# Near-diagonal score levels of a gated linear recurrence computed in blocks of 32 tokens instead of 128

## The chip, the core and the metric

The kernel runs on one core of one Trainium2 chip. The core has a matrix engine (TensorE; PE in the profile, its weight loads PEld), a vector engine (VectorE, DVE), an activation engine (ScalarE, ACT), a general engine (GpSimd, POOL) and a queue that issues transfers (SyncE, SP). Matrix products are written to PSUM, which TensorE alone fills and which DVE and ACT read; everything else lives in SBUF, 128 partitions wide, or in HBM, reached by DMA. The metric is the device time in microseconds of one execution, the median of several.

## The reference, cut to what matters

The program is one layer of a decoder over 16 meta tokens and 1024 tokens (1040 in all), of width 1024: a mixer, and then a gated MLP with a short convolution. Half of the mixer is a gated linear recurrence with 4 heads, keys of 128 and values of 128. The change is in its scores:

```python
def _hgrn2_chunk_step(state, xs):
    q, k, v, lf = xs
    b = jnp.cumsum(lf, axis=2)
    o_inter = jnp.einsum('bhtk,bhkv->bhtv', q * jnp.exp(b), state)
    diff = b[:, :, :, None, :] - b[:, :, None, :, :]
    decay = jnp.where(causal, jnp.exp(jnp.where(causal, diff, 0.0)), 0.0)
    scores = jnp.einsum('bhtk,bhtsk,bhsk->bhts', q, decay, k)
    o_intra = jnp.einsum('bhts,bhsv->bhtv', scores, v)
    k_dec = k * jnp.exp(b_last[:, :, None, :] - b)
    new_state = jnp.exp(b_last)[..., None] * state + jnp.einsum('bhsk,bhsv->bhkv', k_dec, v)
    return new_state, o_inter + o_intra
```

The decay between a query t and an earlier key s is different in each of the 128 key channels, so the scores aren't one matrix product. Outside this function stand the projections that give q, the forget gate, the values and the gates; a causal pooling branch; two branch projections; an output projection; and the MLP.

## The kernel before, in words

**The scores by levels.** The kernel takes chunks of P = 128 tokens, NCH = 8 of them behind the meta tokens. Inside a chunk it splits the pairs (t, s) by levels 2, 4, 8, 16, 32 and 64. At level lv the tokens are cut into blocks of 2·lv; the second half of a block holds queries, the first half keys, and both are scaled by the decay from the block's middle. So one tile holds scaled keys and scaled queries interleaved, and a product of it with itself has the wanted scores in some places. What the levels leave (the diagonal and its direct neighbour) is the base, a product of keys and queries.

**Scores on TensorE (`head_steps`).** For levels 2 to 16 `level_mm` makes for each chunk one product of all 128 columns of the chunk (as weights) with its 64 query columns (L833), 8 of them into one bank of PSUM, 128x512. `level_out` picks the wanted places out of it with one predicated copy on DVE through a mask of bytes (L849, 128x512 elements), into the head's score array `sc`, 128x1024, that POOL has set to zero (L803). For levels 32 and 64 each product is made for the wanted block alone: weights 32 or 64 columns wide, written at partitions 0 and 64, or at 0 (L829); a plain copy on ACT or DVE sets them into `sc` (L843; the list `ON_ACT` says which are ACT's). The base is 8 products of 128 by 128 per head (L890), in two banks, with one predicated copy of 128x512 for each bank (L891). One product in float32 shows in the trace as two weight loads and two matmuls. Later steps of the head make the states (L899, L906), and the outputs from `sc` and the values, and from the states (L928, L929).

**What the levels get.** Cumulated logarithms `b` come from a scan on DVE: for heads 0 and 1 nine scans of a chunk each (L673), for heads 2 and 3 one scan over 1040 elements with an array `keep_on` that is zero where a chunk begins (L669). A level's tile then takes a subtraction (L750), two exponentials on ACT (L753, L754) and two products with q and k (L756, L757). Heads 0 and 1 have this done early, by `prepare`, during the gate projections, and stored to HBM (`hscr`); `head_steps` loads the tiles again (L691). Heads 2 and 3 do it in place. The list `POOLED` says which of these operations go to POOL; the others go to DVE.

**Order.** After the gate projections the work follows the list `ORDER`: `p1` is a step of `prepare`, `F2` the forget-gate projection of head 2 (`Fa2`, `Fb2` its two halves), `c2` its chain of logarithms, `Q..` the query projection, `h0` the next of the 12 or 13 steps of head 0, `l`, `w` loads and early weight splits of later stages, `BB0..7` and `BA0..7` the two branch projections, `sa` the split of a head's output. Inside this stage the program order is the list's, and a planner with its own costs places the instructions on the engines' queues; SP's queue issues in order. A `BB` result with more than SPILL_OVER = 4 `h` steps behind it in the list is stored to HBM (L1372) and loaded again for its `BA` (L1358). Large tiles come from a pool of 27 slots.

Of the kernel before, what the change touches and what calls it, by code (L numbers as in the profile page):

```python
# [41 lines left out]
LUP = 2.0 ** 60  # L42
KT = 6
HT = 514
HN = HT - HALO
# [16 lines left out]

ORDER = ("p1 p1 p1 p1 h0 F2 p1 h0 p1 h0 p1 Qa2 p1 p1 p1 p1 p1 h0 h0 c2 h1 w1 Qb2 h0 w0 Fa3 h1 h0 h2 h0 h0 h2 w4 h1 "
         "h0 h1 h1 h2 l0 Fb3 w4 c3 h1 h0 Q3 h0 h2 h2 h1 h3 h1 w4 l1 h2 h2 l2 l3 h1 h1 w2 h3 BB0 h2 h2 h3 h2 w5 BB1 "
         "h3 h1 BB2 h3 BB3 w5 h1 h3 BB4 h3 h2 BB5 w3 sa1 h3 h3 h3 sa0 h2 BB6 h3 h1 w5 h2 BB7 sa2 w5 h3 sa3 BA1 BA5 "
         "BA6 BA2 BA4 h3 BA0 BA3 BA7")
POOLED = ("e1k.0 e1k.3 kdsub.2 lk32.1 lk4.1 lq32.1 lq64.3 lq8.0 osg.2 wBA2 wBA6 wBA7 wBB2 wF0 wF3 wPP2 wPV0 wPV1 "
          "wQ0 qsmul.1 lq2.1 wQ2 sub2.3 lk32.3 lq4.2 sub8.0 lq32.0 lk64.1 sub8.3 lk2.1 qsmul.0 sub4.2 lq8.3 lq32.3 "
          "lk16.1 lq2.0 lk8.1 sub32.2 lf.1 lq4.3 sub4.1 e1q.2 sub2.0 qsmul.3 lq4.0 lk8.3 sub64.1 lq8.2 lq4.1 sub2.2 "
          "lk4.2 e1k.2 e1k.1 wQ3 kdsub.1").split()  # L70
ON_ACT = "lo32.0 lo32.1 lo64.0 lo64.1 lo32.2 lo64.2 lo64.3".split()
SPILL_OVER = 4
# [8 lines left out]
def trunk_kernel(ctx: ExitStack, tc: tile.TileContext, x, meta_tokens, mix_norm_pre,  # L81
# [523 lines left out]
    masks = {}  # L605
    mbase = const.tile([P, P], U8, name="mbase")
    mtmps = slot(P + len(LEVELS) * P // 2, name="mtmps")
# [5 lines left out]
                         pattern=[[2, P // 2], [1, 2]], channel_multiplier=-1)  # L613
    pool_e.tensor_copy(mbase, mtmp)
    for i, h in enumerate(LEVELS):
# [6 lines left out]
        masks[h] = const.tile([P, P // 2], U8, name=f"mask{h}")  # L622
        pool_e.tensor_copy(masks[h], mt)

# [32 lines left out]
    def chain_steps(h, kk, b, f, f2):  # L657
# [9 lines left out]
        eng(f"lf.{h}").tensor_tensor(f, f, f2, ALU.add)  # L667
        if ("F", h) not in FIRST_JOBS:
            dve.tensor_tensor_scan(b, keep_on[0], f, 0.0, ALU.mult, ALU.add)  # L669
        else:  # L670
            for lo in range(NM - P, L, P):
                t = slice(max(lo, 0), lo + P)
                dve.tensor_tensor_scan(b[:, t], ones[:, : t.stop - t.start], f[:, t], 0.0, ALU.mult, ALU.add)  # L673
        heads[h].update(kk=kk, b=b, f=f)
# [114 lines left out]
    def head_steps(h):  # L789
# [11 lines left out]
        if early:  # L801
            q = load_part("q", h)
        pool_e.memset(sc, 0.0)  # L803

        def meta_mm():
# [15 lines left out]
        def level_mm(lv, qk):  # L821
            ps = bank("sl")
            half = lv >= 32
            for c in range(NCH):
                t = NM + c * P
                if half:
                    for i in range(P // (2 * lv)):
                        s, n = t + 2 * lv * i, 2 * lv * i
                        pe.matmul(ps[n : n + lv, c * lv : (c + 1) * lv], qk[:, s : s + lv], qk[:, s + lv : s + 2 * lv],  # L829
                                  start=True, stop=True)  # L830
                    continue
                rhs = qk[:, t : t + P].rearrange("p (b two h) -> p b two h", two=2, h=lv)[:, :, 1, :]
                pe.matmul(ps[:, c * 64 : (c + 1) * 64], qk[:, t : t + P], rhs, start=True, stop=True)  # L833
            return ps

        def level_out(lv, ps):
# [8 lines left out]
            nb = P // (2 * lv)  # L845
            o4 = sc.rearrange("p (c b two h) -> p c b two h", c=NCH, two=2, h=lv)[:, :, :, 1, :]
            p4 = ps.rearrange("p (c b h) -> p c b h", c=NCH, h=lv)
            m4 = masks[lv].rearrange("p (o b h) -> p o b h", o=1, h=lv).to_broadcast([P, NCH, nb, lv])
# [36 lines left out]
        yield  # L885
        for j in range(2):
            ps = bank("sb")
            for i in range(4):
                t = NM + (4 * j + i) * P
                pe.matmul(ps[:, i * P : (i + 1) * P], kk[:, t : t + P], q[:, t : t + P], start=True, stop=True)  # L890
            dve.copy_predicated(sc[:, j * 512 : (j + 1) * 512].rearrange("p (c t) -> p c t", c=4),  # L891
                                mbase.rearrange("p (o t) -> p o t", o=1).to_broadcast([P, 4, P]),
                                ps.rearrange("p (c t) -> p c t", c=4))
        yield
# [1078 lines left out]
```

## Time and profile before

| | |
|---|---|
| median of 3 runs | 1338.39 us (1337.05 to 1339.64) |
| the profiled execution | 1341.08 us, its span 1339.2 us |
| mean granted TensorE clock | 0.993 |
| TensorE busy | 1319.1 us (98%), 7665 matmuls |
| DVE, ACT, POOL busy | 991.3, 610.5, 466.2 us |
| mean DMA traffic | 207 GB/s |
| stage of the heads | about 357 to 590 us of the span |

The row of a group has the line, the engine, the operation, the tile written and read, the shapes and the count; then busy time, mean duration of one, and the idle time before them with what ended it. In a row of the timeline or of the chain stand the start and the length of a run of like instructions; matmuls are pipelined, so a run's length is the spacing of the starts times their number, and a little more. The chain is followed back from the last instruction to what released it.

### The profile page before, as it was taken

How to read it: one execution, taken by the hardware profiler on the slowest of the kernel's cores; microseconds unless marked ns; L12 is line 12 of the kernel's file. 1: busy time of each engine (PE TensorE's matmuls, PEld its weight loads, DVE VectorE, ACT ScalarE, POOL GpSimd, SP SyncE). 2: the span in 40 equal slices, each digit the busy share in tenths (PEclk: the TensorE clock that was granted, in tenths of full speed). 3: DMA queues.
4: the chain of work that ended last, by engine and by line, in shares of the span. 5: the costliest groups of instructions: out<-in, count | busy, mean ns of one | idle time of the engine just before them, and what ended most of it. 6: DMA issues, size and time to landing. Idle time of an engine off the chain costs nothing.

```text
span 1339.2 us, 20195 instructions
## 1 busy us (share of the span) xinstructions
PE 1319.1 (98%) x7665; PEld 1166.1 (87%) x7665; DVE 991.3 (74%) x1260; ACT 610.5 (46%) x985; POOL 466.2 (35%) x348
## 2 busy tenths in 40 slices
PE   8999999999999899999999999999999999999997
PEld 7799999999999899987899888888888888888886
DVE  6761878689666868755669999888889996455757
ACT  5544655555666646424664322222222223354543
POOL 2003462457651322042026555546556652000000
PEclk9999999999989899999999999999999999999999
DMA  8135444464798766887686677776776799676653
GB/s 270 41 120 172 162 165 142 136 208 152 197 352 297 236 222 211 309 309 251 227 310 224 190 213 195 203 205 155 172 163 152 177 230 308 220 228 223 221 188 141
DMA packets 149217, 277.83 MB, mean 207 GB/s; under 512 B 10536, under 2 KB 74700, under 8 KB 149122
## 3 DMA queue, kind: packets, MB, share of 16 engines
q1 hardware_dynamic: 137058, 252.18, 56.1%
q0 software_dynamic: 12064, 24.38, 10.8%
q8 instruction: 60, 0.98, 0.3%
q14 instruction: 35, 0.29, 0.1%
HBM read 189.29 MB, written 110.26 MB: 224 GB/s over the span
## 4 chain that ended last, share of the span: by engine, by line
PE 88%; DMA 5%; ACT 2%; DVE 1%; issue 1%; POOL 1%; SPq 1%; DVEq 0%; POOLq 0%; ACTq 0%
PE P L322 16%; PE P L325 16%; PE P L323 16%; PE pd L198 5%; PE pd L200 5%; PE pd L199 5%; PE sl L833 2%; PE pm L199 2%; PE pm L200 2%; PE pm L198 2%; DMA wraw<-in_w_out_dram 2%; DMA sb<-sscr 1%; PE pv L199 1%; PE pv L200 1%; PE pv L198 1%
## 5 line engine op out<-in xcount | busy, mean ns | idle before, releaser
L322 PE MATMUL P<-v,whi 128*128 128x512 f32 (+2 forms) x408 | 140.8, 352 | 0.0
L323 PE MATMUL P<-v,whi 128*128 128x512 f32 (+2 forms) x408 | 140.5, 352 | 0.0
L325 PE MATMUL P<-v,wlo 128*128 128x512 f32 (+2 forms) x424 | 135.2, 349 | 0.0
L1707 DVE TENSOR_TENSOR rot<-wraw,rot 128x1024 fp32r<-128x1024 f32 x31 | 38.0, 1225 | 72.3 <-ACT rot L1706 72.2
L267 ACT CAST whi<-wraw 128x512 fp32r<-128x512 f32 x90 | 53.0, 618 | 81.7 <-PE P L323 68.4
L268 DVE TENSOR_TENSOR wlo<-wraw,whi 128x512 fp32r<-128x512 f32 x86 | 80.5, 958 | 12.7 <-ACT whi L267 12.7
L293 POOL TENSOR_TENSOR swa<-wraw,wraw 128x512 f32<-128x512 f32 x32 | 50.0, 1564 | 111.2 <-DMA wraw<-in_ffn_w_gate_dram 74.6
L322 PEld LDWEIGHTS P<-v,whi 128*128 128x128 f32 x408 | 76.7, 188 | 10.4
L323 PEld LDWEIGHTS P<-v,whi 128*128 128x128 f32 x408 | 76.6, 188 | 10.3
L325 PEld LDWEIGHTS P<-v,wlo 128*128 128x128 f32 x424 | 74.0, 188 | 11.0
L199 PE MATMUL pd<-rot 128*128 128x512 f32 x272 | 82.1, 389 | 0.0
L200 PE MATMUL pd<-rot 128*128 128x512 f32 x272 | 82.1, 389 | 0.0
L198 PE MATMUL pd<-rot 128*128 128x512 f32 x272 | 81.1, 390 | 0.1
L268 DVE TENSOR_TENSOR wlo<-swb,whi 128x512 fp32r<-128x512 f32 x64 | 71.6, 1125 | 9.0 <-ACT whi L267 9.0
L1706 ACT CAST rot<-wraw 128x1024 fp32r<-128x1024 f32 x31 | 32.7, 1054 | 90.8 <-PE pd L200 89.5
L267 ACT CAST whi<-swa 128x512 fp32r<-128x512 f32 x64 | 38.1, 616 | 76.6 <-PE P L323 71.0
L322 PE MATMUL P<-uhi,whi 128*128 128x258 f32 (+2 forms) x240 | 69.0, 304 | 0.6 <-ACT q L679 0.6
L267 ACT CAST whi<-swb 128x512 fp32r<-128x512 f32 x64 | 38.2, 617 | 67.4 <-PE P L323 63.5
L323 PE MATMUL P<-ulo,whi 128*128 128x258 f32 (+2 forms) x240 | 68.9, 305 | 0.0
L1635 DVE SCALAR_TENSOR_TENSOR y<-g,par,y 128x1024 f32<-128x1024 f32 x44 | 65.6, 1491 | 0.8
L322 PE MATMUL P<-t2h,whi 128*128 128x258 f32 (+2 forms) x228 | 65.3, 304 | 0.2 <-DVE sg L1022 0.2
L322 PE MATMUL P<-t4h,whi 128*128 128x258 f32 (+2 forms) x228 | 64.9, 302 | 0.1
(451 smaller groups left out, 4109.3 us busy)
## 6 DMA issues: line engine op xcount, KB each, us to landing
wraw<-in_w_in_dram SPq DMA_DIRECT2D x36, 512.0 KB, 4.6
yt<-ysum SPq DMA_DIRECT2D x33, 512.0 KB, 4.5
wraw<-in_ffn_w_gate_dram SPq DMA_DIRECT2D x26, 512.0 KB, 7.9
wraw<-in_ffn_w_up_dram SPq DMA_DIRECT2D x22, 512.0 KB, 5.3
wsum<-in_ffn_w_down_dram SPq DMA_DIRECT2D x22, 512.0 KB, 8.6
wraw<-in_w_out_dram SPq DMA_DIRECT2D x18, 512.0 KB, 4.3
ysum<-ys SPq DMA_DIRECT2D x11, 768.0 KB, 7.8
sa<-sscr SPq DMA_DIRECT2D x16, 513.0 KB, 8.5
```

Of the source, the lines that this page charges most:

```text
L198: pe.matmul(ps, ahi, bhi, start=first, stop=False)
L199: pe.matmul(ps, ahi, blo, start=False, stop=False)
L200: pe.matmul(ps, alo, bhi, start=False, stop=last)
L267: act.copy(hi, src)
L268: (pool_e if 4 <= i < 2 * self.early else dve).tensor_tensor(lo, src, rr(hi), ALU.subtract)
L293: pool_e.tensor_tensor(s1, a21, a22, ALU.add)
L322: pe.matmul(d, whi[:, k, :], xh[:, c : c + w], start=(k == 0 and onto is None), stop=False, **go)
L323: pe.matmul(d, whi[:, k, :], xl[:, c : c + w], start=False, stop=False, **go)
L325: pe.matmul(x[:, o : o + w], wlo[:, k, :], xh[:, c : c + w], start=False, stop=(k == 3), **go)
L1635: dve.scalar_tensor_tensor(a, g[:, j : j + SEQ], cvw[:, j, m : m + 1], a, ALU.mult, ALU.add)
L1706: act.copy(hi, src)
L1707: dve.tensor_tensor(lo, src, rr(hi), ALU.subtract)
```

## The change

Levels 2 to 16 and the base are made per block of BLK = 32 tokens. All their pairs lie inside such a block. The product of 128 weight columns with 64 (base: 128) moving columns becomes four, of 32 weight columns with 16 (base: 32), written at partitions 0, 32, 64 and 96. Their results go into a narrow array `dg`, 32 columns per chunk instead of 128, a quarter of a tile `dgs` that the four heads share: the predicated copies are 128x128 (levels) and 128x256 (base, now one bank). After the base, four copies of 32x256 set `dg`'s blocks onto the diagonal of `sc`: 12 of the 16 on ACT (`lodg..` in `ON_ACT`), the others on DVE. POOL sets `dg` to zero too. The masks are narrow and made by small copies at the start; the masks of levels 32 and 64, which nothing reads, go.

`keep_on` goes, and its slot is `dgs`'; heads 2 and 3 get the nine scans. The copy of level 64 of head 1 moves from ACT to DVE. `POOLED` loses e1k.1, e1k.2, e1k.3, kdsub.1, kdsub.2, lf.1, lk64.1, lq4.2, lq64.3, osg.2, sub2.2, sub4.2 and wQ0 (to DVE, but wQ0 names nothing that is made), and gains kdmul.3, lf.0, lq16.3, lq32.2, sub16.1, sub16.2, sub64.2 (dg3.1 is on `ON_ACT`, which goes first).

`ORDER` is rearranged: six `p1` instead of four ahead of the first `h0`; `F2` is split with its first half ahead of that `h0`, and `Q3` is split; `c2` comes earlier; `BB6` has 4 `h` steps behind it instead of 5, so its result is no longer stored and loaded again.

```diff
+BLK = 32
-ORDER = ("p1 p1 p1 p1 h0 F2 p1 h0 p1 h0 p1 Qa2 p1 p1 p1 p1 p1 h0 h0 c2 h1 w1 Qb2 h0 w0 Fa3 h1 h0 h2 h0 h0 h2 w4 h1 "
+ORDER = ("p1 p1 p1 p1 p1 p1 Fa2 h0 Fb2 h0 p1 h0 Qa2 p1 p1 p1 p1 c2 h0 h0 h0 w1 w0 h1 Qb2 Fa3 h1 h0 h2 h0 h0 h2 h2 "
...
-ON_ACT = "lo32.0 lo32.1 lo64.0 lo64.1 lo32.2 lo64.2 lo64.3".split()
+ON_ACT = "lo32.0 lo32.1 lo64.0 lo32.2 lo64.2 lo64.3 lodg0.0 lodg0.1 lodg0.2 lodg0.3 lodg1.0 lodg1.1 lodg1.2 lodg2.2 lodg2.3 lodg3.1 lodg3.2 lodg3.3".split()
...
-        if ("F", h) not in FIRST_JOBS:
-            dve.tensor_tensor_scan(b, keep_on[0], f, 0.0, ALU.mult, ALU.add)
-        else:
-            for lo in range(NM - P, L, P):
+        for lo in range(NM - P, L, P):
+            t = slice(max(lo, 0), lo + P)
+            dve.tensor_tensor_scan(b[:, t], ones[:, : t.stop - t.start], f[:, t], 0.0, ALU.mult, ALU.add)
...
+        dg = dgs[:, h * NCH * BLK : (h + 1) * NCH * BLK]
         pool_e.memset(sc, 0.0)
+        pool_e.memset(dg, 0.0)
...
-                rhs = qk[:, t : t + P].rearrange("p (b two h) -> p b two h", two=2, h=lv)[:, :, 1, :]
-                pe.matmul(ps[:, c * 64 : (c + 1) * 64], qk[:, t : t + P], rhs, start=True, stop=True)
+                for n in range(0, P, BLK):
+                    k = qk[:, t + n : t + n + BLK]
+                    rhs = k.rearrange("p (b two h) -> p b two h", two=2, h=lv)[:, :, 1, :]
+                    pe.matmul(ps[n : n + BLK, c * BLK // 2 : (c + 1) * BLK // 2], k, rhs, start=True, stop=True)
...
-        for j in range(2):
-            ps = bank("sb")
-            for i in range(4):
-                t = NM + (4 * j + i) * P
-                pe.matmul(ps[:, i * P : (i + 1) * P], kk[:, t : t + P], q[:, t : t + P], start=True, stop=True)
-            dve.copy_predicated(sc[:, j * 512 : (j + 1) * 512].rearrange("p (c t) -> p c t", c=4),
-                                mbase.rearrange("p (o t) -> p o t", o=1).to_broadcast([P, 4, P]),
-                                ps.rearrange("p (c t) -> p c t", c=4))
+        ps = bank("sb")
+        for c in range(NCH):
+            for n in range(0, P, BLK):
+                t = NM + c * P + n
+                pe.matmul(ps[n : n + BLK, c * BLK : (c + 1) * BLK], kk[:, t : t + BLK], q[:, t : t + BLK], start=True,
+                          stop=True)
+        d3 = dg.rearrange("p (c t) -> p c t", c=NCH)
+        dve.copy_predicated(d3, mbase.rearrange("p (o t) -> p o t", o=1).to_broadcast([P, NCH, BLK]),
+                            ps[:, : NCH * BLK].rearrange("p (c t) -> p c t", c=NCH))
+        for n in range(0, P, BLK):
+            r = slice(n, n + BLK)
+            o3 = sc[r].rearrange("p (c t) -> p c t", c=NCH)[:, :, r]
+            if f"lodg{n // BLK}.{h}" in ON_ACT:
+                act.copy(o3, d3[r])
+            else:
+                eng(f"dg{n // BLK}.{h}").tensor_copy(o3, d3[r])
...
-    keep_on = [slot(L, name="keep_on")]
-    pool_e.memset(keep_on[0], 1.0)
-    pool_e.memset(keep_on[0][:, NM:].rearrange("p (c t) -> p c t", t=P)[:, :, :1], 0.0)
+    dgs = slot(HEADS * NCH * BLK, name="dgs")
```

More of the change, by code (lines that the diff above doesn't have):

```diff
@@ L61 @@
 AHEAD = 3
-ORDER = ("p1 p1 p1 p1 h0 F2 p1 h0 p1 h0 p1 Qa2 p1 p1 p1 p1 p1 h0 h0 c2 h1 w1 Qb2 h0 w0 Fa3 h1 h0 h2 h0 h0 h2 w4 h1 "
[L64 to L70, printed above, removed]
-ON_ACT = "lo32.0 lo32.1 lo64.0 lo64.1 lo32.2 lo64.2 lo64.3".split()
+ORDER = ("p1 p1 p1 p1 p1 p1 Fa2 h0 Fb2 h0 p1 h0 Qa2 p1 p1 p1 p1 c2 h0 h0 h0 w1 w0 h1 Qb2 Fa3 h1 h0 h2 h0 h0 h2 h2 "
[3 rows of a table added]
+POOLED = ("e1k.0 lk32.1 lk4.1 lq32.1 lq8.0 wBA2 wBA6 wBA7 wBB2 wF0 wF3 wPP2 wPV0 wPV1 qsmul.1 lq2.1 wQ2 sub2.3 "
+          "lk32.3 sub8.0 lq32.0 sub8.3 lk2.1 qsmul.0 lq8.3 lq32.3 lk16.1 lq2.0 lk8.1 sub32.2 lq4.3 sub4.1 e1q.2 "
+          "sub2.0 qsmul.3 lq4.0 lk8.3 sub64.1 lq8.2 lq4.1 lk4.2 wQ3 lq16.3 sub16.2 kdmul.3 lq32.2 lf.0 dg3.1 "
+          "sub64.2 sub16.1").split()
+ON_ACT = "lo32.0 lo32.1 lo64.0 lo32.2 lo64.2 lo64.3 lodg0.0 lodg0.1 lodg0.2 lodg0.3 lodg1.0 lodg1.1 lodg1.2 lodg2.2 lodg2.3 lodg3.1 lodg3.2 lodg3.3".split()
 SPILL_OVER = 4
@@ L605, in trunk_kernel @@
     masks = {}
-    mbase = const.tile([P, P], U8, name="mbase")
+    mbase = const.tile([P, BLK], U8, name="mbase")
     mtmps = slot(P + len(LEVELS) * P // 2, name="mtmps")
@@ L613, in trunk_kernel @@
                          pattern=[[2, P // 2], [1, 2]], channel_multiplier=-1)
-    pool_e.tensor_copy(mbase, mtmp)
-    for i, h in enumerate(LEVELS):
+    for n in range(0, P, BLK):
+        r = slice(n, n + BLK)
+        pool_e.tensor_copy(mbase[r], mtmp[r, r])
+    for i, h in enumerate(LEVELS[:4]):
         mt = mtmps[:, P + i * P // 2 : P + (i + 1) * P // 2]
@@ L621, in trunk_kernel @@
                              pattern=[[2 * h, P // (2 * h)], [0, h]], channel_multiplier=-1)
-        masks[h] = const.tile([P, P // 2], U8, name=f"mask{h}")
-        pool_e.tensor_copy(masks[h], mt)
+        masks[h] = const.tile([P, BLK // 2], U8, name=f"mask{h}")
+        for n in range(0, P, BLK):
+            r = slice(n, n + BLK)
+            pool_e.tensor_copy(masks[h][r], mt[r, n // 2 : (n + BLK) // 2])
     def V(c, h):
```

10 lines of the change are left out of this document (6 added, 4 removed), and 3 rows, old and new, of the table ORDER.

## The prediction

> **What bounds the kernel now.** I read the page first, then busy time by stretch around the heads, then TensorE's waits there, then the rows of the instructions that the change touches.
>
> ```profile
> span 1339.2 us, 20195 instructions
> PE 1319.1 (98%) x7665; PEld 1166.1 (87%) x7665; DVE 991.3 (74%) x1260; ACT 610.5 (46%) x985; POOL 466.2 (35%) x348
> ```
>
> TensorE is busy 98% of the span, so time taken off its queue is the first candidate for a gain. The stretches say whether it is the bound where the change lies (columns: length, busy time and instructions of PE, PEld, DVE, ACT, POOL, then granted clock, DMA share, GB/s):
>
> ```profile
> 355.00:375.00 20.00, 17.07 (x110) 16.40 (x109) 7.95 (x6) 11.77 (x19) 18.01 (x12) 0.91 1.08 305
> 375.00:400.00 25.00, 25.00 (x182) 24.75 (x182) 21.29 (x16) 15.90 (x23) 12.71 (x7) 0.86 0.96 340
> 440.00:460.00 20.00, 17.17 (x160) 16.16 (x159) 17.20 (x23) 17.73 (x31) 7.08 (x5) 0.83 0.89 262
> 560.00:590.00 30.00, 29.54 (x185) 29.02 (x184) 22.68 (x40) 6.60 (x16) 7.99 (x5) 1.00 0.84 316
> 371.50:600.00 228.50, 222.87 (x1635) 214.37 (x1636) 166.03 (x227) 123.49 (x199) 61.93 (x36) 0.96 0.80 274
> ```
>
> Over the heads (last line) TensorE works 222.87 of 228.50 us, DVE 166.03, ACT 123.49, POOL 61.93. TensorE is the bound, with two dents: in 355 to 375 and in 440 to 460 it stands idle some 3 us each, and the granted clock falls there or right behind (0.91 and 0.86, then 0.83). The largest waits in the dents:
>
> ```profile
> PE sl L829 <- DVE d L757: 2.2, 1, 2.2
> PE sm L808 <- DMA rq<-hscr: 1.5, 1, 1.5
> PE sl L833 <- DMA r<-hscr: 1.0, 1, 1.0
> ```
>
> Head 0 waits for tiles read back from HBM (1.5 + 1.0 us), and a level of a later head for its inputs from DVE (2.2 us).
>
> **The change on TensorE.** The rows of the products that change, and of those that have the new form already (level 32: 32 weight columns, at two places in turn):
>
> ```profile
> L833 PE MATMUL sl<-r x128: 219/275/472, 372.4 to 423.3; 128*128 128x64 f32 x128
> L833 PE MATMUL sl<-d x128: 217/275/326, 414.1 to 494.6; 128*128 128x64 f32 x128
> L829 PE MATMUL sl<-r x96: 196/196/270, 395.5 to 446.9; 128*32 128x32 f32 x64, 128*64 128x64 f32 x32
> ...
> 372.40 7.09 PE sl L833 x32
> 386.31 3.52 PE sl L833 x32
> 395.53 0.63 PE sl L829 x32
> 396.16 0.36 PE pf L218
> 396.52 0.16 PE pf L219
> 520.58 1.79 PE sb L890 x16
> ...
> 395.46 0.70 PE L829 MATMUL sl<-r 128*32 128x32 f32 x32
> 406.36 1.15 PE L829 MATMUL sl<-r 128*64 128x64 f32 x16
> 451.14 1.07 PE L829 MATMUL sl<-d 128*32 128x32 f32 x32 [2.23 <-DVE d L757]
> ```
>
> The first three lines give counts and durations (least, median, most, ns), the next six are pieces of the chain (start, us), the last three are runs of the timeline. A level of a head is 16 matmuls of L833: 32 take 3.52 us at full clock, so a level 1.76 and a matmul 0.110. A base, 16 of L890, takes 1.79. So 128 moving columns cost what 64 do: the weights set the pace. The narrow form: 0.70 us for 32, less one's own 0.196, over 31 steps, is 16.3 ns from start to start. In the chain that burst takes 0.63, and the matmul behind it 0.36 where its neighbour takes 0.16; the 0.63 holds some 0.11 beside 32 x 16.3 ns. I charge 0.11 + 0.20 = 0.31 to each burst as its edge.
>
> A new level is 64 narrow matmuls: 64 x 0.0163 + 0.31 = 1.35 us, so -0.41 against 1.76. A new base is the same 64: -0.44 against 1.79. Four levels and a base in four heads: 16 x 0.41 + 4 x 0.44 = 8.3 us less on TensorE.
>
> The spacing is the one number that the trace doesn't show for this form: four places in turn, and 64 in one burst. From below: two places overlap in the row of 16.3; if four did, it would be 8 ns, a burst 0.82, and the change -18.7 us. From above: the 64-wide row has one place, so nothing overlaps; (1.15 - 0.222) / 15 is 62 ns, hence about 31 for 32 columns; a burst is then 2.29 and the change 16 x 0.53 + 4 x 0.50 = +10.5 us. It is even at (1.76 - 0.31) / 64 = 22.7 ns. I take 16.3, from the row that is nearest: same width, two passes, places in turn. Nor does the row with half the clock speak against it: 1.07 us for 32 at 451.14, where L833 took 7.09 for two levels at 372.40. If the slow stretches stay under the same levels, each of two gains some 0.9 more, and a base as much; that -2.7 is in the range, not in the sum.
>
> The Trainium skill, in TensorE: Matmul & The Clock Gate, section "Wait — 56ns, not 53.3ns?", says that matmuls never start closer than about 25 ns however small they are. By this rule a new level would be an estimated 64 x 0.025 + 0.31 = 1.91 us and the sum +2.9 us instead of -8.3. The trace disagrees for bursts of 32 (16.3 ns), and no run here shows a longer narrow burst.
>
> **The change on the other engines.**
>
> ```profile
> L849 DVE COPY_PREDICATED sc<-mask,sl x16: 690/718/1305, 376.2 to 495.1; 128x512 f32<-128x512 uint8 x16
> L891 DVE COPY_PREDICATED sc<-mbase,sb x8: 723/729/737, 413.1 to 525.7; 128x512 f32<-128x512 uint8 x8
> L843 ACT COPY sc<-sl x10: 346/364/579, 397.9 to 511.5; 32x256 f32<-32x256 f32 x6, 64x512 f32<-64x512 f32 x4
> L843 DVE COPY sc<-sl x2: 405/414/422, 503.5 to 503.9; 32x256 f32<-32x256 f32 x2
> L669 DVE TENSOR_TENSOR_SCAN b<-keep_on,f x2: 2325/3138/3951, 392.8 to 434.4; 128x1040 f32<-128x1040 f32 x2
> L673 DVE TENSOR_TENSOR_SCAN b<-ones,rf x18: 185/401/418, 151.6 to 317.2; 128x128 f32<-128x128 f32 x16, 128x16 f32<-128x16 f32 x2
> L750 DVE TENSOR_TENSOR d<-b x15: 1211/1220/3435, 176.9 to 495.7; 128x1024 f32<-128x1024 f32 x15
> L750 POOL TENSOR_TENSOR d<-b x9: 1893/2017/2901, 155.7 to 472.0; 128x1024 f32<-128x1024 f32 x9
> L757 DVE TENSOR_TENSOR d<-d,kk x9: 670/680/1927, 400.6 to 502.9; 128x512 f32<-128x512 f32 x9
> L803 POOL MEMSET sc<- x4: 947/949/966, 357.8 to 444.4; 128x1024 f32 x4
> ```
>
> DVE: an element costs (1220 - 680) / 512 = 1.05 ns between the subtraction and the product. A level's copy of 128 instead of 512 elements is then 718 - 403 = 315 ns: 16 times -0.40 is -6.5 us. The base: one copy of 256, 0.46, for two of 0.729: -1.0 in each head, -4.0. Added are four diagonal copies at 0.41 (+1.6), level 64's copy of head 1 (+0.7, from the 0.718 of 512 elements out of PSUM), and nine scans for one: 8 x 0.401 + 0.185 = 3.4 against 2.3 to 4.0 us, +0.5 for both heads (at most +2.1). The new `POOLED` gives DVE three e1k and three lk or lq (6 x 0.68), two kdsub, lf, osg and two sub (6 x 1.22), 11.4, and takes three sub, kdmul and lf (5 x 1.22) and two lq (2 x 0.68), 7.5: +3.9. In sum -3.8 of 166: no bound.
>
> ACT gets 12 copies of 0.35 and loses one pair of level 64 (0.58): +3.6 on 123. They stand behind the predicated copy of the base, and what queues behind them on ACT are the copies of states and outputs. Their reader is the output product, two steps after the base; the time between is the states' products and whatever stands in `ORDER` there. The last base ends at 520.58 + 1.79, and that head's outputs start 8.8 us later (last row below), against a tail of 0.46 + 4 x 0.4 = 2.1. Free while that cover stands; without it, 2 us a head. POOL is relieved by some 8 us by `POOLED` (a sub is 2.02 there), pays four memsets of a quarter of 0.949, and saves the one of `keep_on`; the masks are made in the first 10 us and first needed at 372. All free.
>
> DMA and SP's queue: `BB6` is no longer stored and loaded again. The rows of its transfers, of SP's waits, of `F2`'s first matmul and the first of head 0, and of the chain:
>
> ```profile
> L1372 SPq DMA_DIRECT2D sscr<-sa x7: 319/320/1997, 473.2 to 534.4; - x7
> L1358 SPq DMA_DIRECT2D sb<-sscr x7: 319/457/976, 551.8 to 566.5; - x7
> SPq L691 <- DMA hscr<-rq: 2.8, 1, 2.8
> SPq L720 <- POOL d L757: 9.8, 3, 5.6
> ...
> 357.34 0.32 PE L218 MATMUL pf<-uhi,whi 128*128 128x348 f32 x1
> 371.14 0.25 PE L808 MATMUL sm<-rq,em 128*16 128x2 f32 x4 [1.47 <-DMA rq<-hscr]
> ...
> 364.59 7.77 DMA r<-hscr
> 531.13 0.53 PE po L920 x4
> ```
>
> One store and one load fewer of seven. TensorE hardly waits around them (29.54 of 30 us busy in 560 to 590), so I count nothing; it holds one more slot until `BA6`. The two extra `p1` put up to two more stores of head 1 ahead of head 0's first loads in SP's queue, and such stores waited 9.8 us for POOL in three cases. `F2` used to cover those loads whole; now only its second half lies between the load and its use. I count nothing for that either, as the split moves the load's place without saying when its slot is free; the price is in the first rival. Nor do I count a change at the two dents.
>
> Sum: 1341.08 - 8.3 = 1332.8 for an execution like the profiled one. That one is 2.7 us over the median, so in terms of the median it is 1338.39 - 8.3 = 1330.1.
>
> **The rivals.** First, on the other side: head 0's first level tiles come later. TensorE then has only half of `F2` (half of the 13 us from 357.3 to 371.1, less small waits) between load and use, so up to 6.7 us more idle, and the clock falls for longer: L833 took 7.09 instead of 3.52 us for two levels in the slow stretch, which is half speed, and the granted 0.91 and 0.86 are 3.6 + 7.0 us at half speed, which lose 5; another such stretch loses 5 more. So +11.7 on -8.3: 1341.8, slower. It decides from 8.3 us of new loss on. For it: 7.77 us from issue to landing, SP's waits for POOL, DMA share over 1 in 355 to 375. Against: the load's issue waited for an earlier store (2.8 us), not for `F2`, so it may go out as early as before.
>
> Second: long narrow bursts don't keep the spacing of short ones. At 25 ns the time is 1341.3, at 31 ns 1348.9; even at 22.7. For it: no burst over 32 in the trace. Against: the even 16.3 ns within that burst.
>
> Third, better: four places overlap, or the dents close (2.5 us of waiting and 5 of slow clock in the one, 2.2 and 3.4 in the other). 1338.4 - 18.7 = 1319.7, or 1338.4 - 8.3 - 7.5 = 1322.6 with one dent gone.
>
> Fourth: TensorE gets lighter but the end of the stage doesn't come earlier, as the loads for the `BA` projections set it. DMA is 0.84 busy in 560 to 590. Then nearly all is lost: 1337. Against: TensorE's busy 29.54 of 30 there.
>
> **How the numbers follow.** The forecast as summed, 1325 to 1335.5: 0.50. Third: 0.13. First: 0.17, of which I give half to losses over 2.7 us. Second: 0.08, most of it slower. Fourth and mishaps of the new order: 0.12, half within 0.2%. A difference under 0.2%, 2.7 us, can't be told from no change here. Faster: 0.50 + 0.13 + 0.03 of the first = 0.66; slower 0.09 + 0.06 + 0.05 = 0.20; the rest, 0.14, the same. The range 1318 to 1343 reaches to the third and the first; 31 ns lies outside.
>
> **What would show it.** Right: 1024 matmuls of the levels instead of 256 and 256 of the base instead of 64, 14 to 18 ns apart, a level's burst about 1.35 us; predicated copies of some 0.3 and 0.46 us on DVE; six loads at L1358; TensorE's busy time 8 us lower with no new wait over 2 us. Wrong: a spacing over 22 ns; a longer wait for `r<-hscr` at the first levels, with a longer slow stretch; a wait of the output product for the diagonal copies.

## The result and the profile after

The changed kernel takes 1337.76 us (median of 20 runs, 1334.60 to 1340.67), the kernel before 1339.55 us (20 runs, 1334.74 to 1342.79). The ratio is 0.9983 with a 95% interval of 0.9974 to 0.9992: 1.8 us less, inside the 0.2% that the prediction called no change. The forecast was 1330.1, 8.3 us less than before; some 2 of these 8 us came.

The head of the page of the changed kernel, and its row of the chain that ended last:

```profile
span 1337.5 us, 22156 instructions
PE 1299.5 (97%) x8625; PEld 1143.7 (86%) x8625; DVE 981.8 (73%) x1284; ACT 612.8 (46%) x995; POOL 454.4 (34%) x350
PE 84%; DMA 7%; DVE 4%; ACT 2%; issue 2%; POOL 1%; SPq 0%; DVEq 0%; ACTq 0%
```

The same chain row of the kernel before:

```profile
PE 88%; DMA 5%; ACT 2%; DVE 1%; issue 1%; POOL 1%; SPq 1%; DVEq 0%; POOLq 0%; ACTq 0%
```

TensorE is busy 1299.5 us instead of 1319.1: 19.6 us less, more than twice the forecast, and the span is 1.7 us shorter. In the chain TensorE's share falls by 4 points, and those of DMA and DVE rise by 5 together.

Where it went shows in the stage of the heads, cut at the first matmul of the forget gate (`pf`), the first of a branch projection (`pbb`) and the first behind the stage (`pm`). Stretches of the kernel before, with the columns given in the prediction:

```profile
357.30:461.50 104.20, 98.43 (x782) 95.65 (x780) 74.06 (x81) 70.83 (x111) 42.18 (x27) 0.92 0.89 286
461.50:588.40 126.90, 125.02 (x883) 121.94 (x882) 93.89 (x144) 57.03 (x90) 26.93 (x15) 1.00 0.74 256
```

And of the changed kernel, cut at the same matmuls:

```profile
357.80:460.00 102.20, 83.47 (x1502) 78.76 (x1500) 63.33 (x101) 68.17 (x109) 35.30 (x24) 0.88 0.88 292
460.00:587.20 127.20, 120.73 (x1132) 116.19 (x1122) 93.63 (x147) 62.43 (x103) 22.54 (x13) 1.00 0.76 255
```

In the first part TensorE does 15.0 us less work (98.43 to 83.47) and the part gets 2.0 us shorter; in the second 4.3 us less, and it gets 0.3 longer. Together 19.2 us of work went and 1.7 us of time: TensorE's idle time in the stage grew from 7.7 to 25.2 us. The granted clock is a little lower in the first part (0.88 against 0.92); what this costs is inside the busy time, so the 19.2 us are net of it. What stands behind the stage is as long as before (1339.2 - 588.4 = 750.8, and 1337.5 - 587.2 = 750.3).

The stretches of the changed kernel that answer to those of the prediction:

```profile
355.00:375.00 20.00, 15.66 (x165) 14.89 (x163) 9.82 (x10) 12.69 (x22) 19.09 (x14) 1.00 1.05 308
375.00:400.00 25.00, 21.34 (x317) 20.75 (x318) 14.54 (x26) 15.55 (x22) 4.25 (x3) 0.80 1.03 368
440.00:460.00 20.00, 14.27 (x367) 12.80 (x365) 16.28 (x22) 17.56 (x29) 5.63 (x4) 0.83 0.85 274
560.00:590.00 30.00, 29.29 (x181) 28.39 (x179) 23.80 (x34) 6.60 (x16) 9.27 (x5) 1.00 0.81 316
```

The two dents are wider: in 355 to 375 TensorE now stands idle 4.3 us (2.9 before), in 375 to 400 3.7 (0), in 440 to 460 5.7 (2.8). In 375 to 400 the clock fell too, 0.80 against 0.86. TensorE's waits in the stage, changed kernel (line waited at, what released it; us in total, times, longest). Line numbers are each kernel's own: here L839 makes the narrow products, and L833 those of levels 32 and 64.

```profile
PE sl L833 <- DVE d L759: 5.7, 1, 5.7
PE sl L839 <- issue: 5.0, 2, 4.1
PE sl L833 <- DMA r<-hscr: 3.6, 1, 3.6
PE sl L839 <- DMA r<-hscr: 2.2, 2, 1.2
PE sm L812 <- DMA rq<-hscr: 1.8, 1, 1.8
PE pbb L219 <- DMA phi<-pscr: 1.6, 1, 1.6
PE pbb L219 <- ACT rs L954: 1.4, 1, 1.4
PE pbb L220 <- DMA plo<-pscr: 1.2, 1, 1.2
PE po L944 <- DVE st L924: 1.1, 1, 1.1
```

There is no single new wait. The largest shows how a gain is lost. This is TensorE's timeline of the changed kernel (start and length of a run; in brackets the idle time before it and its releaser):

```profile
373.14 0.74 PE L839 MATMUL sl<-r 128*32 128x16 f32 x64 [0.99 <-DMA r<-hscr]
375.07 1.06 PE L839 MATMUL sl<-r 128*32 128x16 f32 x64 [1.19 <-DMA r<-hscr]
382.96 1.32 PE L839 MATMUL sl<-r 128*32 128x16 f32 x128
411.60 0.73 PE L897 MATMUL sb<-rq,rkk 128*32 128x32 f32 x62
412.26 1.23 PE L839 MATMUL sl<-d 128*32 128x16 f32 x114
417.57 0.35 PE L839 MATMUL sl<-d 128*32 128x16 f32 x10 [4.08 <-issue]
451.13 1.07 PE L833 MATMUL sl<-d 128*32 128x32 f32 x32 [5.73 <-DVE d L759]
```

The last row is a level 32 in its own place. In the prediction's row of the kernel before it started at 451.14 after 2.23 us of waiting for the same product on DVE; now at 451.13 after 5.73. TensorE came 3.5 us sooner to an input that came no sooner. That input is the end of a row of work on ACT which TensorE itself starts. When the query projection `pq` is done, ACT makes `q` (from 441.32 before, from 441.55 now); behind it stand two table loads of 1.28 us each, `rs` and the exponentials. From the first `pf` to there it takes 84.0 us before and 83.8 now, with TensorE busy 81.07 and 70.80 us. So 10 us of the saving were lost already, to the loads of head 0 (7.6 us of waits against 2.5) and to the waits named issue (5.0 against none). The rows at 373.14 and 375.07 are the same at head 0: two levels that took 7.09 us in one run before are now short, and each waits for its tile from HBM.

The rows of the instructions that changed (least, median, most in ns):

```profile
L839 PE MATMUL sl<-r x512: 176/183/236, 373.1 to 425.0; 128*32 128x16 f32 x171
L856 DVE COPY_PREDICATED dgs<-mask,sl x16: 286/299/445, 374.0 to 496.5; 128x128 f32<-128x128 uint8 x16
L900 DVE COPY_PREDICATED dgs<-mbase,sb x4: 428/443/454, 412.5 to 523.4; 128x256 f32<-128x256 uint8 x4
L906 ACT COPY sc<-dgs x12: 388/403/407, 414.4 to 524.9; 32x256 f32<-32x256 f32 x12
L908 DVE COPY sc<-dgs x4: 283/284/290, 414.9 to 524.7; 32x256 f32<-32x256 f32 x4
```

From the run at 382.96: (1.32 - 0.18) / 127 = 9.0 ns from start to start, where the prediction took 16.3. The base, at 411.60, has 32 moving columns like the row of 16.3, and (0.73 - 0.20) / 61 = 8.7 ns. So it is the four places, and not the 16 moving columns, that go with the closer spacing.

### The profile page after: what moved, and what is told of

Read it like the earlier page. It is cut to its first block, busy times and chain, and to the rows that moved or that the text cites. A ratio compares the mean times of both kernels' runs of the same rounds, so it can differ in the third digit from the quotient of the medians.

```text
span 1337.5 us, 22156 instructions
## 1 busy us (share of the span) xinstructions
PE 1299.5 (97%) x8625; PEld 1143.7 (86%) x8625; DVE 981.8 (73%) x1284; ACT 612.8 (46%) x995; POOL 454.4 (34%) x350
## 4 chain that ended last, share of the span: by engine, by line
PE 84%; DMA 7%; DVE 4%; ACT 2%; issue 2%; POOL 1%; SPq 0%; DVEq 0%; ACTq 0%
PE P L323 16%; PE P L326 16%; PE P L324 16%; PE pd L199 5%; PE pd L201 5%; PE pd L200 5%; PE pm L199 2%; PE pm L201 2%; PE pm L200 2%; DMA sscr<-sa 1%; PE pv L200 1%; PE pv L199 1%; PE pv L201 1%; PE pg L219 1%; PE pg L223 1%
## 5 line engine op out<-in xcount | busy, mean ns | idle before, releaser
L269 DVE TENSOR_TENSOR wlo<-wraw,whi 128x512 fp32r<-128x512 f32 x86 | 83.4, 992 | 12.7 <-ACT whi L268 12.7
L294 POOL TENSOR_TENSOR swa<-wraw,wraw 128x512 f32<-128x512 f32 x32 | 46.9, 1466 | 106.9 <-DMA wraw<-in_ffn_w_gate_dram 71.7
L324 PE MATMUL P<-t4l,whi 128*128 128x258 f32 (+2 forms) x228 | 64.9, 303 | 0.0
```

The source lines that it names most:

```text
L269: (pool_e if 4 <= i < 2 * self.early else dve).tensor_tensor(lo, src, rr(hi), ALU.subtract)
L294: pool_e.tensor_tensor(s1, a21, a22, ALU.add)
L324: pe.matmul(d, whi[:, k, :], xl[:, c : c + w], start=False, stop=False, **go)
```

## The experiments

Three theories. Hidden chains (second limit, slack or sides in the expectations): what TensorE saved was taken up by work on the other engines and queues that stood just behind it. Lists: the new order and placement cost what the products save. Supply: the four times as many narrow products come too slowly to TensorE. Times are medians, and ratios are to the kernel before on the same chip.

**One half of the change at a time.** `blocks_old_lists`: the products and copies per block, with the order and placements of before.

`ORDER` and `POOLED` are those of before, and `ON_ACT` is that of before with the 12 `lodg` names:

```diff
-ON_ACT = "lo32.0 lo32.1 lo64.0 lo32.2 lo64.2 lo64.3 lodg0.0 lodg0.1 lodg0.2 lodg0.3 lodg1.0 lodg1.1 lodg1.2 lodg2.2 lodg2.3 lodg3.1 lodg3.2 lodg3.3".split()
+ON_ACT = "lo32.0 lo32.1 lo64.0 lo64.1 lo32.2 lo64.2 lo64.3 lodg0.0 lodg0.1 lodg0.2 lodg0.3 lodg1.0 lodg1.1 lodg1.2 lodg2.2 lodg2.3 lodg3.1 lodg3.2 lodg3.3".split()
```

> The blocks of 32 tokens with the lists of before: ORDER, POOLED and ON_ACT as before, the twelve diagonal copies on ScalarE as in the change. Nothing is left out. Three theories for where the 19.6 us that TensorE is busy less have gone (the time fell by 1.8). Lists: the rearranged lists made the new waits; then this kernel keeps most of the gain, 1321 to 1328 us. Second limit: the transfers and the chains of DVE and ACT stood just behind TensorE in the stage of the heads, whatever the lists; then 1333 to 1341. Instruction supply: narrow bursts run the instruction buffer empty (5.0 us of waits named issue, and a slow clock behind them); then 1333 to 1341 too, and the waits named issue are here again, 3 us or more.

1344.66 us, ratio 1.0050 [1.0035, 1.0065]. `new_lists_wide` is the other half, the kernel before with the three lists of the changed one:

> The kernel before, with products over 128 tokens, and the lists of the change (the names of the diagonal copies name nothing here). Nothing is left out. Lists: the new lists cost it 8 us or more, 1346 and above. Second limit and instruction supply: about the time of before, 1336 to 1342, with no wait named issue inside a burst of the levels.

1344.32 us, ratio 1.0047 [1.0031, 1.0064]. Each half alone costs some 6 us, and both together gain 1.8. Neither time lies in a range that a theory gave for it. But the new lists don't eat the products' gain: without them the products lose. The largest waits of TensorE with the old lists:

```profile
PE sl L839 <- issue: 7.1, 2, 3.7
PE pt L886 <- DMA rkd<-hscr: 4.6, 2, 3.4
PE sl L833 <- DVE d L759: 3.8, 2, 3.1
PE po L935 <- issue: 3.4, 1, 3.4
```

The stops named issue and the wait for DVE's product are those of the changed kernel; the read-back of `rkd` and the stop at the outputs (L935) are new. The idle time in the stage is 31.4 us. How far does a small difference in the lists alone move the time? `one_op_moved` takes one subtraction of head 3 from POOL to DVE:

```diff
-POOLED = ("e1k.0 lk32.1 lk4.1 lq32.1 lq8.0 wBA2 wBA6 wBA7 wBB2 wF0 wF3 wPP2 wPV0 wPV1 qsmul.1 lq2.1 wQ2 sub2.3 "
+POOLED = ("e1k.0 lk32.1 lk4.1 lq32.1 lq8.0 wBA2 wBA6 wBA7 wBB2 wF0 wF3 wPP2 wPV0 wPV1 qsmul.1 lq2.1 wQ2 "
```

> The changed kernel with one name taken off POOLED: the subtraction of level 2 of head 3 goes from POOL (2.0 us) to DVE (1.2 us). Nothing is left out. A control for how far the planner's order moves the time by itself. If the planner's order is worth little: within 1.5 us of the change, 1336 to 1339. If any edit draws another order, worth some 6 us as in the runs with the lists exchanged: 1341 and above, with other waits than in the change.

1337.50 us, ratio 0.9994 [0.9980, 1.0007], as expected of a planner's order that is worth little. TensorE's waits inside the stage sum to 24.0 us, against 24.5 in the changed kernel (the 25.2 above less 0.7 ahead of the first `pm`; so summed below too). A new placement by itself need not move the time. Still, each edit below also makes the planner place other work differently, so that a few us can't be laid to one edit.

**The supply.** `supply_alone` adds a bench ahead of the kernel's work, to a bank that nobody reads:

```diff
+        for i in range(512):
+            n = 32 * (i % 4)
+            pe.matmul(junk_bank[n : n + 32, :16], ones[:, n : n + 32], ident[:, n : n + 16], start=True, stop=True)
+        for _ in range(64):
+            pe.matmul(junk_bank[:, :64], ones, ident[:, :64], start=True, stop=True)
+        for i in range(256):
+            pe.matmul(junk_bank[:32, :16], ones[:, :32], ident[:, :16], start=True, stop=True)
...
-        warm(14)
+        warm(64)
+        bench()
```

> The kernel before with matmuls of constants put at its start, into a bank that nothing reads (50 more warm ones first): 512 narrow products as in the change (32 weight columns, 16 moving, four places in turn), then 64 wide ones (128 and 64), then 256 narrow ones at one place. Nothing waits for data, and no transfers of weights run yet beside the loads of the start. Each product is two matmuls and two weight loads. Instruction supply: the first stretch starts at about 9 ns a matmul and then stops, again and again, as 2048 instructions pass in some 9 us; its mean is 15 ns or more, some 15 us for 1024 matmuls. If the two long waits named issue have another cause: 9 ns throughout, 9 us, with no gap over 0.2 us. The wide stretch is 128 x 0.112 = 14 us by both, the narrow one at one place 512 x 0.025 to 0.031 = 13 to 16 us.

Its time, 1435.45 us, is that of the added work and says nothing else. Rows of the narrow products in TensorE's timeline, and the stretches of the narrow, the wide and the one-place products:

```profile
18.25 2.05 PE L541 MATMUL pj<-ident,ones 128*32 128x16 f32 x223
23.67 1.90 PE L541 MATMUL pj<-ident,ones 128*32 128x16 f32 x128 [3.37 <-issue]
32.23 1.90 PE L541 MATMUL pj<-ident,ones 128*32 128x16 f32 x128 [1.55 <-issue]
```

```profile
18.00:47.00 29.00, 14.14 (x1025) 13.31 (x1026) 0.00 (x0) 0.00 (x0) 0.00 (x0) 0.59 0.32 94
47.00:74.00 27.00, 27.00 (x144) 26.96 (x136) 0.00 (x0) 0.00 (x0) 0.00 (x0) 0.50 0.01 1
74.00:103.00 29.00, 29.00 (x521) 28.85 (x521) 0.00 (x0) 0.00 (x0) 0.00 (x0) 0.50 0.01 2
```

The first 223 start (2.05 - 0.18) / 222 = 8.4 ns apart. Then TensorE stops after every 128, for 1.55 to 3.37 us, and waits for nothing that the trace shows but its own issue. 1024 take 28.8 us, 28 ns each. 128 matmuls with their 128 weight loads are 256 instructions. The queue that brings instructions moved 1.21 MB in 74 packets, 16 KB each; in the kernel before it moved 60. That is 14 packets more for 3528 instructions more (23723 and 20195 in all), 252 to a packet. A stop at each such block is the likely reading; that the stop is the fetch isn't shown. So a long run of narrow products is set by its supply, as the supply theory expected. Short runs between wide matmuls mostly aren't: the changed kernel has two such stops of some size (5.0 us in its waits).

Do these set its time? `quarter_products` makes a quarter of the narrow products, each with one chunk's keys and four chunks' queries (the base likewise):

```diff
                 for n in range(0, P, BLK):
+                    if c % 4:
+                        continue
                     k = qk[:, t + n : t + n + BLK]
-                    rhs = k.rearrange("p (b two h) -> p b two h", two=2, h=lv)[:, :, 1, :]
-                    pe.matmul(ps[n : n + BLK, c * BLK // 2 : (c + 1) * BLK // 2], k, rhs, start=True, stop=True)
+                    rhs = qk[:, t : t + 4 * P].rearrange("p (c t) -> p c t", t=P)[:, :, n : n + BLK]
+                    rhs = rhs.rearrange("p c (b two h) -> p c b two h", two=2, h=lv)[:, :, :, 1, :]
+                    pe.matmul(ps[n : n + BLK, c * BLK // 2 : (c + 4) * BLK // 2], k, rhs, start=True, stop=True)
```

> The changed kernel, but each narrow product takes the weights of one chunk and the queries of four, so that a quarter of the narrow instructions is issued for the same columns of PSUM (the scores of three chunks in four are left wrong; all copies and transfers are as in the change). TensorE is lighter by some 9 us more. Instruction supply: the waits named issue (5.0 us) and the slow clock behind them go, 1328 to 1333 us. Second limit: 1335 to 1338.5, as nothing that waited for data comes sooner. Lists: as second limit.

1345.53 us, ratio 1.0051 [1.0036, 1.0067]: all theories missed. Its largest waits:

```profile
PE sl L833 <- DMA r<-hscr: 7.0, 1, 7.0
PE ms L957 <- ACT rh L1023: 6.2, 3, 2.2
```

No wait for issue is left, and others stand there, 30.6 us in the stage. `blocks_of_64` goes half the way, with two blocks a chunk, which is half the matmuls; level 32 goes into `dg` too, and `dgs` takes two slots:

```diff
-BLK = 32
+BLK = 64
...
-    dgs = slot(HEADS * NCH * BLK, name="dgs")
+    dgs = [slot(2 * NCH * BLK, name="dgs") for _ in range(2)]
```

> The changed kernel with blocks of 64 tokens: half as many products, 64 weight columns wide, two places; level 32 lies inside the block and is set into the narrow array too, the diagonal copies are 8 of 64x512, the narrow arrays take two slots instead of one. Nothing is left out. 64 matmuls of a level and head become 32; from the row of two places I expect some 29 ns each, 0.9 us a level instead of 0.56, so 7 us more on TensorE. Instruction supply: 128 matmuls now take 3.7 us, as long as a fetch cycle of 3.5 us, the waits named issue (5.0 us) and the slow clock of 416 to 423 us go: 1329 to 1336. Slack: 1336 to 1343.

1341.00 us, ratio 1.0026 [1.0013, 1.0039], again with no wait for issue; its largest is

```profile
PE ms L953 <- ACT rh L1019: 10.5, 2, 7.8
```

which is in the second part of the stage; the first branch projection starts at 460.1, as in the changed kernel. The supply costs the change its 5 us of waiting, but neither kernel without those stops was faster; the time of `blocks_of_64` is in the range of slack. Neither is a clean test, as TensorE is busy 1302.5 and 1306.7 us in them, more than the 1299.5 of the changed kernel; `quarter_products` had been expected to be 9 us lighter.

**One chain at a time.** `read_once_narrow` lets heads 0 and 1 load three of their six level tiles, and use each for two levels:

```diff
+        pend_ = []
...
+                if lv in (4, 16, 64):
+                    return pend_[0]
-                return load_part(lv, h)
+                pend_[:] = [load_part(lv, h)]
+                return pend_[0]
```

> The changed kernel, but heads 0 and 1 read one level's tile back from HBM for each pair of levels instead of two (the second level of a pair is computed from the first one's tile, so its scores are left wrong): six reads of 0.5 MB fewer, some 3 MB, 8 to 9 us of DMA at the 368 GB/s of that stretch. Second limit: the waits for read tiles at the first levels (7.5 us in all) mostly go, 1329 to 1334 us. Instruction supply and lists: 1335 to 1339.

1337.04 us, ratio 0.9998 [0.9983, 1.0013]: not the gain of the second limit. The waits for tiles read back are still 5.6 us (7.6 in the changed kernel). `one_pooled_narrow` loads the pooled branch's results once and uses them for all four groups:

```diff
+        if phi.count(None) < len(phi):
+            phi[g], plo[g] = next((p, l) for p, l in zip(phi, plo) if p is not None)
+            return
```

> The changed kernel, but the pooled branch is loaded from HBM once instead of four times and used for all four groups (its product is wrong): six loads of 0.5 MB and six slots fewer before the first branch projection. In all kernels so far that projection starts at 460 to 463 us of the span, though TensorE's work before it differs by 15 us and more. Theory slots: that start is set by the slots for these loads, which come free behind the chains of the heads on DVE. Then it starts 5 us or more earlier here and the time is 1328 to 1333 us. Rival, chains: the projections only fill in what the heads leave free, the heads' own steps set the end; then the first projection may move but the time stays within 1334 to 1339.

1334.73 us, ratio 0.9983 [0.9966, 0.9999], and the first branch projection starts at 458.3, 1.7 us sooner: chains, and not slots. `one_pooled_wide` is the same edit on the kernel before:

> The same edit on the kernel before. Slots: there TensorE is the bound by a small margin, so the time falls by 0 to 4 us, 1335 to 1340. Chains: 1337 to 1341.

1337.32 us, ratio 1.0000 [0.9984, 1.0017], inside both ranges. `light_levels_narrow` leaves the products with q and k out of the levels of heads 2 and 3:

```diff
+        if h >= 2:
+            return
```

> The changed kernel, but for heads 2 and 3 the two products of a level's tile with q and k are left out (24 operations, 16 of them on DVE with 0.68 us each, 8 on POOL with 1.3 each; the scores are wrong): some 11 us less on DVE and a shorter way from exponentials to TensorE. Chains: the time falls by 4 us or more against the change, 1326 to 1334. Slots: within 1334 to 1339.

1337.70 us, ratio 0.9997 [0.9978, 1.0017]: here chains missed. No chain alone gives back anything that can be told from nothing: the ratios are 0.9998, 0.9983 and 0.9997, and the change itself has 0.9983. The waits in the stage of the three narrow ones sum to 23.2, 23.4 and 22.7 us: when one wait goes, the next takes its place.

`relieved_narrow` and `relieved_wide` make the three edits together, on the changed kernel and on the one before:

> The changed kernel with three reliefs at once: one level's tile read for each pair of levels in heads 0 and 1, the pooled branch read once instead of four times, and no products of the levels' tiles with q and k in heads 2 and 3 (scores and pooled branch are wrong). Theory, the sides hold it together: with all of them out of the way the light TensorE shows, and the time falls by 6 us or more against the change, to 1331 or below, more than any relief alone gave (3). Rival, something else holds it (the norm of the outputs and its table loads on ACT, the weights prepared for later, the instructions): 1332 to 1338.

> The same three edits on the kernel before. Sides together: TensorE is the bound here, so the time falls by 0 to 4 us against before, 1334 to 1338.5, and lies 4 us or more above relieved_narrow. Rival: both fall alike, by 0 to 5 us, and lie within 3 us of each other.

1332.33 us (0.9957 [0.9942, 0.9971]) and 1339.32 us (1.0006 [0.9992, 1.0021]). Against the change the narrow one gains 3.5 us by the ratios (0.9957 and 0.9983), and not the 6 or more of sides together; its time lies at the lower end of the range of the rival, that something else holds it. What sides together said of the difference between the two did come. With three side chains lighter, the narrow form is worth 7.0 us instead of 1.8. The wide kernel, forecast to gain 0 to 4, gains nothing from the same relief, which fits with TensorE as its bound. But the narrow one keeps waits, and with them most of the 19.6 us that its form saves on TensorE:

```profile
PE ms L959 <- ACT rh L1028: 7.1, 1, 7.1
PE sl L840 <- DMA r<-hscr: 4.5, 1, 4.5
PE sl L846 <- issue: 3.1, 2, 1.9
```

They sum to 21.6 us in the stage.

**Work put back.** `wide_added` adds four of the eight wide products of each level, into columns that nobody reads:

```diff
+                if c % 2 == 0:
+                    rhs = qk[:, t : t + P].rearrange("p (b two h) -> p b two h", two=2, h=lv)[:, :, 1, :]
+                    pe.matmul(ps[:, 256 + c * 32 : 256 + c * 32 + 64], qk[:, t : t + P], rhs, start=True, stop=True)
```

> The changed kernel with work added on TensorE alone: at each level 4 of the 8 wide products of before are made too, into columns of the same bank that nothing reads: 16 levels x 8 matmuls x 0.110 = 14.1 us of TensorE. Theory slack: behind the lighter TensorE stand chains of other engines and transfers, so that TensorE waits 24.5 us in the stage; the added work fills waits, and the time rises by 0 to 6 us against the change (1337 to 1344). Rival, TensorE is still the bound and the lost gain lies in the waits for instructions and the slow clock: the time rises by 10 us or more (1347 and above), unless the wide products give the instructions time to arrive; then the waits named issue are under 2 us.

1354.66 us, ratio 1.0121 [1.0106, 1.0136].

```profile
PE 1331.0 (98%) x8753; PEld 1169.5 (86%) x8753; DVE 986.0 (73%) x1284; ACT 613.4 (45%) x995; POOL 452.5 (33%) x350
```

TensorE is busy 31.5 us more than in the changed kernel, over twice the 14.1 that the products alone come to (16 x 8 x 0.110): they were put between the narrow ones, so that the form changes many times in a burst, which is likely the reason and isn't shown. The time grows by 16.9 us, as the rival of slack had it (10 us or more); but both had counted on 14.1 us of added work. The waits in the stage fall from 24.5 to 9.7, so they took in about half of what was put back.

**The base and the beginning.** `base_wide` leaves the base as before, so that the diagonal copies come ahead of it:

```diff
-        ps = bank("sb")
-        for c in range(NCH):
...
-                pe.matmul(ps[n : n + BLK, c * BLK : (c + 1) * BLK], kk[:, t : t + BLK], q[:, t : t + BLK], start=True,
-                          stop=True)
...
+        for j in range(2):
+            ps = bank("sb")
+            for i in range(4):
+                t = NM + (4 * j + i) * P
+                pe.matmul(ps[:, i * P : (i + 1) * P], kk[:, t : t + P], q[:, t : t + P], start=True, stop=True)
```

> The changed kernel with the base as before (wide products, two predicated copies into the score array), the diagonal copies ahead of it; the levels stay in blocks. Nothing is left out. TensorE gets 4 x 0.9 = 3.6 us more, a fifth of the narrow instructions go. Instruction supply: the long wait at 412 us, which follows a base and two levels back to back, gets shorter or goes: 1331 to 1336. Slack: 1336 to 1342.

1353.74 us, ratio 1.0114 [1.0098, 1.0129]. Its two largest waits:

```profile
PE sl L831 <- DVE d L757: 7.7, 2, 5.8
PE sl L831 <- DVE wraw L1097: 7.5, 1, 7.5
```

Both forecasts missed. Both waits name DVE, which the wide base gives some 4.1 us more work (eight copies of 0.729 for four of 0.443). The time is 16 us longer; the rest of that isn't explained. `old_start` gives the order its old beginning:

```diff
-ORDER = ("p1 p1 p1 p1 p1 p1 Fa2 h0 Fb2 h0 p1 h0 Qa2 p1 p1 p1 p1 c2 h0 h0 h0 w1 w0 h1 Qb2 Fa3 h1 h0 h2 h0 h0 h2 h2 "
+ORDER = ("p1 p1 p1 p1 h0 F2 p1 h0 p1 h0 p1 Qa2 p1 p1 p1 p1 p1 c2 h0 h0 h0 w1 w0 h1 Qb2 Fa3 h1 h0 h2 h0 h0 h2 h2 "
```

> The changed kernel with the list's beginning as before (four steps of preparation, head 0's first step, the whole of F2, and so on up to Qa2). Nothing is left out. My first rival: the waits for head 0's tiles in 370 to 394 us (7.5 us) are the new beginning's; then they fall to 3 us or less, and the time by up to 5 us, 1333 to 1336. If they come from the lighter TensorE, which reaches the loads earlier, they stay at 5 us or more and the time at 1336 or above.

1339.44 us, ratio 1.0018 [1.0004, 1.0033]. The waits for head 0's level tiles:

```profile
PE sl L833 <- DMA r<-hscr: 4.6, 1, 4.6
PE sl L839 <- DMA r<-hscr: 2.1, 2, 1.3
```

6.7 us, against 5.8 with the new beginning; the wait for `rq` (1.8) is gone, so head 0's waits come to 6.7 in all, against 7.6. So the new beginning doesn't make these waits, as they stay at more than 5 us; by the expectation this speaks for a TensorE that gets to the loads sooner.

## Why the prediction failed

**TensorE's sum: right in kind, too small.** The spacing was the disputed number: 16.3 ns, with bounds of 8 and 31. The 9.0 ns measured lies near the lower bound of 8, where four places overlap, and two levels often share one burst and one edge. With it TensorE's saving is 19.6 us and not 8.3; the bound had said 18.7. The Trainium skill, in TensorE: Matmul & The Clock Gate, section "Wait — 56ns, not 53.3ns?", has about 25 ns as the least from start to start; the 9.0 ns here and the 8.4 ns of the bench speak against it for products at four places in turn. The third rival, which came from this bound, had the work right and the time wrong: it gave 1319.7.

**The step that failed: the saving carried one for one to the time, with everything else costed at nothing.** "TensorE is the bound, with two dents" fits the kernel before, and `relieved_wide` too. But in those dents TensorE already waited for others, and the prediction took work off it there and wrote "Nor do I count a change at the two dents". Each wait there is the place where another chain ends: the read-back of head 0's tiles, and the level of a later head on DVE. A chain that ends when TensorE arrives bounds how much sooner TensorE can go on. At 451 us it shows: the same instruction starts at 451.14 and at 451.13, as the row of work on ACT that it waits for began at 441.3 and 441.6, behind a projection that the earlier waits had held up. Of 19.2 us of work taken away, 17.5 came back as idle time. By releaser, the rows of the stage after, with those of before in the prediction, give most of it: `r` and `rq` from HBM 2.5 to 7.6, DVE's product 2.2 to 5.7, issue none to 5.0. The last of these isn't a chain of another engine; the prediction has such a cost only as a wider spacing, in its second rival.

**Head 0's loads (first rival).** The waits are longer by 5.1 us, and the clock in 375 to 400 lower. Its mechanism, the new beginning of the list, is refuted by `old_start`. The loads stand in stretches with a DMA share of 1.05 and 1.03 (1.08 and 0.96 before).

**Long bursts (second rival).** Inside a burst the spacing holds at 9 ns, so its price per product was wrong; but behind the base and 114 matmuls at 412.26 the issue stops for 4.08 us. In the bench the cost is a stop every 128 matmuls and no wider spacing, and bursts of 64 between wide matmuls mostly escape it.

**The stage's end (fourth rival).** That TensorE gets lighter and the stage hardly ends sooner came out, at 1337.8 for the 1337 it gave. Its place didn't: in 560 to 590 TensorE is 29.29 of 30 us busy, much as before. Most of the gain is gone by 460 us, where the first branch projection starts only 1.5 us sooner behind 15.0 us less work; the 4.3 us of the second part are lost behind that.

**The small terms.** The predicated copies were put at 0.315 and 0.46 us and took 0.299 and 0.443; a diagonal copy at 0.35 to 0.41 took 0.403 on ACT and 0.284 on DVE. No wait of an output product for a diagonal copy shows; the 1.1 us at L944 is for the update of a state (L924). DVE's whole sum was put at -3.8 us, and DVE is busy 9.5 us less (991.3 to 981.8); it wasn't the bound. The `BB6` result is no longer stored, and no wait near 560 came of it.

**Open.** Which chain is next isn't settled: relieving three at once left 21.6 us of waits in the stage. The chain that ended last names one that no run relieves, the stores of weights split early (the `w` jobs in `ORDER`): DVE waits 2.0 us behind `kept5l`, ACT 4.8 behind `kept7h`. In the changed kernel these rows stand in the chain, 27.9 us together:

```profile
431.81 5.17 DMA kept5l<-wlo
445.66 8.93 DMA kept6l<-wlo
478.99 4.83 DMA kept7h<-whi
485.09 5.48 DMA kept3h<-whi
524.20 3.49 DMA kept7h<-whi
```

In the kernel before only two of them do, with 8.5 us (5.36 at 493.48 and 3.12 at 544.93). Whether lighter stores would give the gain back is untested. Each edit also redraws the planner's order, and the runs don't part the two.

## What to carry to other kernels

An engine that is busy 98% of the time isn't for that reason the only bound: read what its few waits end on, and forecast a saving only up to the slack of those chains, stretch by stretch. If the same instruction starts at the same time before and after while its wait grows, follow its input back to where the time went. Where an edit is a set of products with lists fitted to them, measure each half alone before judging either: here each cost 6 us, and together they gained 2.

## What the runs showed of the hardware

Matmuls with 32 weight columns at four places in turn start 8.4 to 9.0 ns apart, with 16 moving columns and with 32, against 16.3 at two places. In a long run of them TensorE stopped after 223 and then after every 128, for 1.55 to 3.37 us each.

The clock can stay low under full load. In the one run of the bench, whose operands are ones and the identity, TensorE was busy 27.00 of 27 us with the wide products (128 weight and 64 moving columns), and 29.00 of 29 with narrow ones at one place, at a granted 0.50 all the time. The Trainium skill, in TensorE: Matmul & The Clock Gate, section "What's actually happening", says that some 3.4 us of sustained work bring full speed; these two rows disagree. In the stage of the heads the clock fell in 375 to 400 where waits and narrow products stand together; which of the two does it isn't parted.
